# Key and value columns of two heads in one 512-column matmul

## The chip, the cores and the metric

The kernel runs on one core of a Trainium2 chip. The metric is the device time of one launch in microseconds (us), and the kernel before takes 2609.01 us, the median of three runs (2603.92 to 2610.87). TensorE (PE) multiplies; its weight loads have a row of their own in the profile (PEld). VectorE (DVE) and ScalarE (ACT) do the elementwise work, GpSimd (POOL) a little of it, and SyncE (SP) issues the transfers of the weights. PE writes its sums into eight banks of 512 fp32 columns, which DVE and ACT read.

## The reference, cut to what matters

Two layers run one after the other on 256 tokens of width 2048. The first has a modulation (adaln) of the norms, neighbourhood attention over 256 latent and 256 context tokens, an output projection and a convolutional FFN. The second has an mLSTM, a latent causal attention and gated output projections. The change is in the first attention's projections:

```python
def project(t):                                  # t: h (256 tokens), then hc (256 tokens)
    q, k, v = jnp.split(t @ w_qkv, 3, axis=-1)   # w_qkv is 2048 x 6144
    sh = (t.shape[0], t.shape[1], NA_HEADS, HEAD_DIM)          # 16 heads of 128
    return rms_norm(q.reshape(sh), q_g), rms_norm(k.reshape(sh), k_g), v.reshape(sh)
q, k, v = project(h)
qc, kc, vc = project(hc)
...
s_lat = einsum('bqhd,bkhd->bhqk', qb, kb) * scale + bias       # masked outside the window
s_ctx = einsum('bqhd,bchd->bhqc', qb, kc) * scale
p = softmax(concatenate([s_lat, s_ctx], -1))
o = einsum('bhqk,bkhd->bqhd', p[..., :nk], vb) + einsum('bhqc,bchd->bqhd', p[..., nk:], vc)
```

Everything is fp32. The kernel splits each fp32 operand into a high and a low part and sums three products (high by high, high by low, low by high).

## The kernel before, in words

**Units of weights.** Every weight matrix is laid out in blocks of 1 MB. A `Unit` (L179) is one block: SP loads it into one of three `raw` tiles, ACT copies it to a rounded tile `whi`, and DVE subtracts to get `wlo`. That is done in two halves ("subs") of 128x1024, each in one of five pairs of buffers, up to four subs ahead of PE (`AHEAD`). Between them stand "rest" units, whose weights (`w_ada`) DVE multiplies and sums into `acc` without PE.

**The projections.** `na_units` (L973) lists the units. The eight pairs of heads are eight groups. Group 0 is woven into the adaln units. For each of groups 1 to 7 there are two units for the keys (`na_k`, L762), two for the values (`na_v`, L818) and two for the queries (`na_q`, L842). Keys and values are needed for 512 tokens, four tiles of 128, and queries for two tiles. `GemmX` (L492) keeps a token tile of `hH` or `hL` as the stationary operand and streams the 256 weight columns of the two heads: `mm3` (L259) issues three matmuls of 256 columns for each of 16 depth steps and each token tile. Two token tiles share a bank. So one group has 16 x 4 x 3 = 192 matmuls for the keys, as many for the values and 96 for the queries.

**After a product.** A key tile is squared on ACT for its norm (`evac` in `na_k`). When all four are done, `chain` runs once per head: DVE and ACT compute the norm's factors (`rsqrt`), ACT copies the four scaled tiles to `kx`, PE transposes them, ACT copies the transposed tile to `k` and DVE takes its low part. The banks of the keys come free when both heads' copies to `kx` are done. A value tile goes to `v` in two pieces, one per head, by ACT and DVE. The queries take a like path (`na_qnorm`, L852), and then `na_attn` (L892) computes scores, softmax, transposes of `p`, and the product with `v`, while the projections of the next group run.

**What sets the order.** Nothing is scheduled on the chip: each engine has a fixed list of instructions. A planner writes the lists while it builds the program. It keeps a clock of its own for PE (`self.now`), ACT and DVE, with costs per instruction. The product of the unit at hand is written in pieces, and at each `yield` of its body the planner looks (`poll`, L382) whether any other piece of work is due by its clock, and writes that next. For the projections the `yield` stands after a token tile of a sub, 12 matmuls. `bank()` (L243) takes a free bank; where none is free, `need` (L230) first writes the work that will free one.

**After the projections** the first weights of the output projection (`wo_units`, L1115) follow. `o_split` (L1109) turns the heads that are done from `oF` into `o`, high and low, on ACT and DVE; PE needs them in the order of the heads.

Of the kernel before, what the change touches and what calls it, by code (L numbers as in the profile page):

```python
# [78 lines left out]
def blocks():  # L79


    t = {}

    def grid(name, K, kt, spans):
        for span in spans:
            for k0 in range(0, K, kt):
                t.setdefault(name, []).append((k0, min(kt, K - k0), span if isinstance(span[0], tuple) else (span,)))

    def wide(lo, hi, n=512):
        return [(c, min(n, hi - c)) for c in range(lo, hi, n)]  # L90
    grid("w_ada", KD, 8, wide(0, 2 * D, 256))
    grid("w_ada", KD, 4, wide(2 * D, 6 * D))
    grid("na_w_qkv", KD, 4, [(c, 256) for c in (0, D, 2 * D)])
    grid("na_w_qkv", KD, 8, [(c + 256 * g, 256) for c in (0, D, 2 * D) for g in range(1, 8)])
    for c in (0, FF):
        grid("ffn_w_up", KD, 8, wide(c, c + FF - 128, 256))
        grid("ffn_w_up", KD, 16, [(c + FF - 128, 128)])
    grid("ffn_w_down", KF, 8, wide(0, D, 256))
    grid("w_in_2", KD, 8, wide(0, 2048, 256))
    grid("w_in_2", KD, 4, wide(2048, 4096))  # L100
    grid("w_in_2", KD, 8, wide(4096, 6144, 256) + wide(6160, 9232, 256) + wide(9296, 15440, 256))
    grid("w_uq_2", 4, 4, wide(0, 3072, 384))
    grid("w_ukv_2", 4, 4, wide(0, 4096))
    grid("na_w_o", KD, 4, wide(0, D // 2))
    grid("na_w_o", KD, 8, wide(D // 2, D, 256))
    for name in ("w_a_2", "w_b_2", "w_out_2"):
        grid(name, KD, 8, wide(0, D, 256))
    return t
# [391 lines left out]
        self.k.mm3(self.out[j], xh, xl, self.wcols(hi), self.wcols(lo), b.start(), last)  # L500


def tokens(x, cg):

    return x[cg].rearrange("p (k c) -> p k c", k=4)
# [22 lines left out]
class Model(Kern):  # L528
# [152 lines left out]
    def na_setup(self):  # L681
        nc = self.nc
        p = self.L.push("h")
        self.hH = p.tile([128, KD, 512], F32R, name="hH")
        self.hL = p.tile([128, KD, 512], F32R, name="hL")
        self.h_ready = set()
        p = self.R.push("kqv")
        self.accring = Ring(self, self.p_c, "acc", [128, 512], F32, 1)
        self.qring = Ring(self, p, "q", [128, 2, 512], F32R, 1)
        self.kring = Ring(self, p, "k", [128, 2, 512], F32R, 2)  # L690
        self.ccring = Ring(self, self.p_c, "cc", [128, 32], F32, 8)
        self.vring = Ring(self, p, "v", [128, 2, 4, 128], F32R, 2)
        self.kxring = Ring(self, p, "kx", [128, 512], F32, 2)
        self.tring = self.kxring
        self.sqring = Ring(self, p, "sq", [128, 512], F32, 1)
        self.q, self.k, self.v, self.rq, self.bias = {}, {}, {}, {}, {}
        self.v_ready, self.k_ready, self.q_ready, self.o_ready = {}, set(), set(), set()
        p = self.R.push("nx")
        self.nx = p.tile([128, KD, 512], F32, name="nx")
        self.adaS = [p.tile([4, 256], F32, name=f"adaS{j}") for j in range(2)]  # L700
        self.x_done, self.x_scaled = 0, set()
        self.rawx = p.tile([128, 2048], F32, name="rawx")
# [59 lines left out]
    def na_k(self, heads):  # L762
        n = 128 * len(heads)
        per = 512 // n
        st = {"r": [], "n": 0, "e": 0}

        def done(j, out, b, last):
            if j == 0:
                st["c"] = self.ccring.get()
            if j % per == 0:  # L770
                st["r"].append(self.releaser(b, per * len(heads)))

            def evac():
                yield from self.calm()
                c = st["c"][0]
                junk, i = self.kxring.get()
                for x in range(len(heads)):
                    self.act(junk[:, col(x)], out[:, col(x)], AF.Square, accum_out=c[:, 4 * x + j:4 * x + j + 1])
                self.kxring.put(i)
                yield  # L780
                st["e"] += 1
                if st["e"] == 4:
                    for x in range(len(heads)):
                        self.spawn(chain(x), 0.2 * x)
            st[j] = out
            self.spawn(evac(), 0.2)

        def chain(x):
            c, ci = st["c"]
            cx, cxi = self.ccring.get()  # L790
            yield from self.rsqrt(cx[:, 0:4], c[:, 4 * x:4 * x + 4], HD, cx[:, 4:12])
            yield
            t, i = self.kxring.get()
            for j in range(4):
                self.act(t[:, col(j)], st[j][:, col(x)], AF.Copy, scale=cx[:, j:j + 1])
                st["r"][j // per]()
            self.ccring.put(cxi)
            st["n"] += 1
            if st["n"] == len(heads):
                self.ccring.put(ci)  # L800
            yield
            b = self.bank()
            for j in range(4):
                self.tr(b.t[:, col(j)], t[:, col(j)])
            self.kxring.put(i)
            yield 0.2
            h = heads[x]
            self.k[h] = self.kring.get()
            k = self.k[h][0]
            self.act(k[:, 0], b.t, AF.Copy, scale=self.vec("kg", 0))  # L810
            yield
            self.stt(k[:, 1], b.t, self.vec("kg", 0), k[:, 0].bitcast(F32), ALU.mult, ALU.subtract)
            b.free()
            self.k_ready.add(h)
        return GemmX(self, KD, 4, lambda k, j: (self.hH[:, k, col(j)], self.hL[:, k, col(j)]), lambda w: w, n, done,
                     need=lambda k: self.need(lambda: k in self.h_ready))

    def na_v(self, heads):  # L818
        def done(j, out, b, last):
            if j == 0:  # L820
                for h in heads:
                    self.v[h] = self.vring.get()
            if not hasattr(b, "rel") or j % 2 == 0:
                b.rel = self.releaser(b, 2)

            def evac(rel=b.rel):
                yield from self.calm()
                o = out.rearrange("p (h c) -> p h c", h=2)
                for i, h in enumerate(heads):
                    v = self.v[h][0]  # L830
                    self.A.copy(out=v[:, 0, j], in_=o[:, i])
                yield
                for i, h in enumerate(heads):
                    v = self.v[h][0]
                    self.V.tensor_sub(out=v[:, 1, j], in0=o[:, i], in1=v[:, 0, j])
                    self.v_ready[h] = self.v_ready.get(h, 0) + 1
                rel()
            self.spawn(evac(), 0.2 + 0.3 * j)
        return GemmX(self, KD, 4, lambda k, j: (self.hH[:, k, col(j)], self.hL[:, k, col(j)]), lambda w: w, 256, done,
                     need=lambda k: self.need(lambda: k in self.h_ready))  # L840

    def na_q(self, heads):  # L842
        outs = []

        def done(j, out, b, last):
            outs.append(out)
            if j:
                self.spawn(self.na_qnorm(heads, outs, b), 0.2)
        return GemmX(self, KD, 2, lambda k, j: (self.hH[:, k, col(j)], self.hL[:, k, col(j)]), lambda w: w, 256, done,
                     need=lambda k: self.need(lambda: k in self.h_ready))  # L850

    def na_qnorm(self, heads, outs, b):  # L852

# [36 lines left out]
        return hb, i  # L890

    def na_attn(self, h):  # L892
        self.need(lambda: h in self.k_ready and self.v_ready.get(h) == 4 and h in self.bias)
        hb, hi_ = self.bias.pop(h)
        x = h % 2
        q, k, r = self.q[h][0], self.k[h][0], self.rq[h][0]
# [59 lines left out]
            ss[t].free()  # L956
        yield
        b = self.bank()
        v = self.v[h][0]
        for x in range(4):  # L960
            self.mm3(b.t[:, 0:256], v[:, 0, x], v[:, 1, x], pt[:, 0, x], pt[:, 1, x], x == 0, x == 3)
        self.ptring.put(pti)
        self.vring.put(self.v.pop(h)[1])
        yield 0.2
        if self.oH is None:
            self.A.copy(out=self.oF[:, h], in_=b.t[:, 0:256])
# [6 lines left out]
    def na_units(self):  # L973
# [15 lines left out]
        rest.reverse()  # L989
        for g in range(1, 8):  # L990
            heads = [2 * g, 2 * g + 1]
            for c0, job in ((D, self.na_k(heads)), (2 * D, self.na_v(heads)), (0, self.na_q(heads))):
                for ku in range(2):
                    us.append(Unit(self.source("na_w_qkv", ku * 8, 8, c0 + g * 256, 256), 8, 256, job.body(ku * 8)))
                    for _ in range(min(len(rest), 1 + ku if c0 else 1 - ku)):
                        us.append(rest.pop())

        last = [u for u in us if u.body is not None and u.kt == 4 and u.cols == 256][-1]
        last.post = self.after_h
# [697 lines left out]
    def mla_begin(self):  # L1697
# [10 lines left out]
        self.kring = Ring(self, p, "bk", [128, 2, 512], F32R, 2)  # L1708
        self.qrring = Ring(self, p, "bqr", [128, 2, 256], F32R, 2)
        self.krring = Ring(self, p, "bkr", [128, 2, 256], F32R, 2)  # L1710
        self.vring = Ring(self, p, "bv", [128, 2, 2, 256], F32R, 2)
        self.zring = Ring(self, p, "bz", [128, 256], F32, 6)
        self.sqring = Ring(self, p, "bsq", [128, 2, 2, 192], F32, 2)
# [440 lines left out]
```

## Time and profile before

| what | value |
|---|---|
| median of three runs | 2609.01 us |
| the profiled execution | 2611.98 us |
| its span, first to last instruction | 2610.2 us |
| mean granted TensorE clock | 0.995 |
| PE busy in the span | 2550.1 us (98%) |
| DVE, ACT busy | 1844.4 us (71%), 1420.7 us (54%) |

The span is the profiled execution without 1.8 us around it. A busy time is the union of an engine's instructions; matmuls overlap in their pipeline, so a single one shows 283 ns (256 columns) while the next starts much earlier. How fast PE really goes is read from starts, not from durations. Groups 1 to 7 of the projections run from about 175 to 645 us, with the attention of the groups before written in between.

### The profile page before, as it was taken

The numbers are of one execution on the slowest core, as the hardware profiler recorded it, in microseconds if no ns is written. First come the engines' busy times: TensorE is split into PE (matmuls) and PEld (weight loads), VectorE is DVE, ScalarE is ACT, GpSimd is POOL, SyncE is SP. The second block draws the span as 40 slices with busy tenths as digits, with TensorE's granted clock in tenths as the row PEclk, the third lists the DMA queues.
The fourth block names the chain that finished last, engine by engine and source line by source line (L and its number), as shares of the span: only waits on it lengthen the run. The fifth ranks groups of instructions, "written<-read, shape, count | busy, mean of one in ns | idle before, by whom it ended". The sixth has DMA issues, their size and how long they took to land.

```text
span 2610.2 us, 40676 instructions
## 1 busy us (share of the span) xinstructions
PE 2550.1 (98%) x16038; PEld 2268.7 (87%) x16038; DVE 1844.4 (71%) x3027; ACT 1420.7 (54%) x2617; POOL 241.3 (9%) x263
## 2 busy tenths in 40 slices
PE   4999999999989999999999999999999999999999
PEld 2799999999978888888888888888888888888888
DVE  7987777677677888787555568677665576677664
ACT  5664444344555555555444456667554467775442
POOL 5421111111110000000000050000000000000000
PEclk9999999999999999999999999999999999999999
DMA  7876776676556666666566554554555553345553
GB/s 267 297 259 221 197 247 189 195 221 182 202 183 225 222 230 225 212 232 219 183 210 208 194 191 163 184 186 158 181 187 200 205 175 134 121 142 209 201 202 147
DMA packets 82543, 522.37 MB, mean 200 GB/s; under 512 B 9232, under 2 KB 15376, under 8 KB 23856
## 3 DMA queue, kind: packets, MB, share of 16 engines
q1 hardware_dynamic: 76656, 501.88, 54.1%
q0 software_dynamic: 5696, 17.90, 4.1%
q8 instruction: 126, 2.06, 0.3%
q14 instruction: 65, 0.53, 0.1%
HBM read 511.35 MB, written 8.39 MB: 199 GB/s over the span
## 4 chain that ended last, share of the span: by engine, by line
PE 94%; DVE 4%; ACT 1%; issue 1%; DMA 0%; SPq 0%; DVEq 0%; ACTq 0%
PE bank L256 91%; PE bank L265 2%; DVE wlo L151 2%; DVE hL L151 0%; ACT L149 0%; DMA nx<-in_ctxT_dram 0%; ACT whi L151 0%; SPq L707 0%; DVE hf L151 0%; DVE gb L151 0%; DVE mct L151 0%; DVE cc L151 0%; DVE adaC L151 0%; PE bank L608 0%; DVE acc L151 0%
## 5 line engine op out<-in xcount | busy, mean ns | idle before, releaser
L151 DVE TENSOR_TENSOR wlo<-raw,whi 128x1024 fp32r<-128x1024 f32 (+3 forms) x822 | 983.3, 1208 | 236.4 <-ACT whi L151 232.2
L151 ACT CAST whi<-raw 128x1024 fp32r<-128x1024 f32 (+3 forms) x822 | 830.5, 1021 | 422.4 <-PE bank L256 321.8
L256 PE MATMUL bank<-h,whi 128*128 128x512 f32 (+1 forms) x1696 | 593.9, 395 | 0.0
L256 PE MATMUL bank<-hf,whi 128*128 128x512 f32 x1376 | 485.0, 397 | 2.6 <-DVE hf L151 2.6
L256 PE MATMUL bank<-h,wlo 128*128 128x256 f32 x1680 | 470.7, 280 | 0.0
L256 PE MATMUL bank<-hf,wlo 128*128 128x256 f32 x1376 | 386.9, 281 | 0.0
L256 PEld LDWEIGHTS bank<-h,whi 128*128 128x128 f32 x1696 | 317.2, 188 | 71.9
L256 PE MATMUL bank<-whi,hH 128*128 128x256 f32 x1280 | 367.1, 287 | 0.0
L256 PE MATMUL bank<-whi,hL 128*128 128x256 f32 x1280 | 362.8, 283 | 2.2 <-DVE hL L151 2.2
L256 PE MATMUL bank<-wlo,hH 128*128 128x256 f32 x1280 | 362.8, 283 | 1.2 <-DVE wlo L151 1.2
L256 PEld LDWEIGHTS bank<-h,wlo 128*128 128x128 f32 x1680 | 317.4, 189 | 0.5 <-DVE wlo L151 0.3
L256 PEld LDWEIGHTS bank<-hf,whi 128*128 128x128 f32 x1376 | 259.0, 188 | 64.7 <-DVE hf L151 3.9
L256 PEld LDWEIGHTS bank<-hf,wlo 128*128 128x128 f32 x1376 | 261.1, 190 | 0.0
L256 PEld LDWEIGHTS bank<-whi,hL 128*128 128x128 f32 x1280 | 245.7, 192 | 2.5 <-DVE hL L151 2.4
L256 PEld LDWEIGHTS bank<-wlo,hH 128*128 128x128 f32 x1280 | 245.8, 192 | 2.3 <-DVE wlo L151 1.8
L256 PEld LDWEIGHTS bank<-whi,hH 128*128 128x128 f32 x1280 | 245.7, 192 | 1.0
L256 PE MATMUL bank<-hid,whi 128*128 128x512 f32 x688 | 243.1, 399 | 0.0
L256 PE MATMUL bank<-hid,wlo 128*128 128x256 f32 x688 | 193.2, 281 | 0.0
L151 DVE SCALAR_TENSOR_TENSOR acc<-raw,cs,acc 128x512 f32<-128x512 f32 x240 | 186.8, 778 | 6.8
L256 PEld LDWEIGHTS bank<-hid,whi 128*128 128x128 f32 x688 | 129.3, 188 | 32.2
L151 ACT COPY fold<-bank 128x256 f32<-128x256 f32 x118 | 43.6, 372 | 160.9 <-PE bank L256 158.2
L256 PEld LDWEIGHTS bank<-hid,wlo 128*128 128x128 f32 x688 | 130.0, 189 | 0.0
(334 smaller groups left out, 3695.7 us busy)
## 6 DMA issues: line engine op xcount, KB each, us to landing
raw<-in_w_in_dram SPq DMA_DIRECT2D x120, 1024.0 KB, 4.8
raw<-in_w_ada_dram SPq DMA_DIRECT2D x86, 1024.0 KB, 4.9
raw<-in_ffn_w_up_dram SPq DMA_DIRECT2D x86, 1024.0 KB, 4.9
raw<-in_na_w_qkv_dram SPq DMA_DIRECT2D x42, 1024.0 KB, 4.9
raw<-in_ffn_w_down_dram SPq DMA_DIRECT2D x40, 1024.0 KB, 4.9
raw<-in_na_w_o_dram SPq DMA_DIRECT2D x16, 1024.0 KB, 5.0
raw<-in_w_a_dram SPq DMA_DIRECT2D x16, 1024.0 KB, 5.0
raw<-in_w_b_dram SPq DMA_DIRECT2D x16, 1024.0 KB, 4.9
```

The lines of the kernel that those rows point to most:

```text
L151: r = f(*a, **kw)
L256: self.T.matmul(out, lhsT, rhs, start=start, stop=stop)
L265: self.T.transpose(out, in_, self.con("id"))
```

## The change

The weight blocks of groups 1 to 7 hold 256 key columns and 256 value columns side by side, four depth steps per block. There are four such units a group in place of two for keys and two for values. A new `GemmKV` streams all 512 columns past a stationary token tile: one triple of 512-column matmuls in place of two triples of 256. Each of the four token tiles has a bank of its own, taken when the tile is first reached, and a `yield` stands after every depth step (three matmuls). A bank comes free after three releases: the value piece, and both heads' copies of the key piece. Values of both heads lie in one tile of 256 columns, so a value tile is one ACT and one DVE instruction instead of two of each. Group 0 keeps its separate units with the new value tile. The queries' units are unchanged, and stand behind the four units of their group as before.

```diff
+    grid("na_w_qkv", KD, 8, [(256 * g, 256) for g in range(1, 8)])
+    grid("na_w_qkv", KD, 4, [((D + 256 * g, 256), (2 * D + 256 * g, 256)) for g in range(1, 8)])
...
+class GemmKV(GemmX):
+    def __init__(self, k, K, xs, done, need):
+        super().__init__(k, K, 4, xs, lambda w: w, 512, done, need)
+    def body(self, kbase):
+        def run(k0, nk, hi, lo):
+            if self.banks is None:
+                self.banks = [None] * 4
+            for j in range(4):
+                if self.banks[j] is None:
+                    self.banks[j] = self.k.bank()
+                b = self.banks[j]
+                self.out = {j: b.t}
+                for kk in range(nk):
+                    kc = kbase + k0 + kk
+                    self.nd(kc)
+                    self.step(j, kc, hi[:, kk], lo[:, kk], b, kc == self.K - 1)
+                    yield
+                if kbase + k0 + nk == self.K:
+                    self.done(j, b.t, b, True)
+                    yield
+        return run
...
-        self.vring = Ring(self, p, "v", [128, 2, 4, 128], F32R, 2)
+        self.vring = Ring(self, p, "v", [128, 2, 4, 256], F32R, 1)
...
             for j in range(4):
                 self.act(t[:, col(j)], st[j][:, col(x)], AF.Copy, scale=cx[:, j:j + 1])
-                st["r"][j // per]()
+                st["r"][j]()
...
+    def na_values(self, j, out, heads, rel):
+        g = heads[0] // 2
+        yield from self.calm()
+        if g not in self.v:
+            self.v[g] = self.vring.get()
+        v = self.v[g][0]
+        self.A.copy(out=v[:, 0, j], in_=out)
+        yield
+        self.V.tensor_sub(out=v[:, 1, j], in0=out, in1=v[:, 0, j])
+        self.v_ready[g] = self.v_ready.get(g, 0) + 1
+        rel()
...
+    def na_kv(self, heads):
+        evac = self.na_keys(heads)
+        def done(j, out, b, last):
+            rel = self.releaser(b, 3)
+            self.spawn(self.na_values(j, out[:, 256:512], heads, rel), 0.2)
+            self.spawn(evac(j, out[:, 0:256], rel), 0.3)
+        return GemmKV(self, KD, self.hx, done, self.hneed)
...
-            for c0, job in ((D, self.na_k(heads)), (2 * D, self.na_v(heads)), (0, self.na_q(heads))):
-                for ku in range(2):
-                    us.append(Unit(self.source("na_w_qkv", ku * 8, 8, c0 + g * 256, 256), 8, 256, job.body(ku * 8)))
-                    for _ in range(min(len(rest), 1 + ku if c0 else 1 - ku)):
-                        us.append(rest.pop())
+            job = self.na_kv(heads)
+            for ku in range(4):
+                us.append(Unit(self.source("na_w_qkv", ku * 4, 4, D + g * 256, 512), 4, 512, job.body(ku * 4)))
+                for _ in range(min(len(rest), 1 + ku % 2)):
+                    us.append(rest.pop())
+            job = self.na_q(heads)
+            for ku in range(2):
+                us.append(Unit(self.source("na_w_qkv", ku * 8, 8, g * 256, 256), 8, 256, job.body(ku * 8)))
+                for _ in range(min(len(rest), 1 - ku)):
+                    us.append(rest.pop())
```

**PE, the keys of group 3 (heads 6 and 7).** `kx1` and `kx0` are the scaled keys of the two heads, `cons` the identity for a transpose; the banks carry the planner's numbers. Before, the transposes stand in the middle of the value product:

```order
L256 MATMUL bank0_3795<-whi_3779,hL_107 128x256
L265 MATMUL bank5_4037<-cons_76,kx1_126 128x128 x4
L256 MATMUL bank0_3795<-whi_3779,hH_106 128x256
L256 MATMUL bank0_3795<-wlo_3780,hH_106 128x256
...
L265 MATMUL bank3_4055<-cons_76,kx0_125 128x128 x4
L256 MATMUL bank1_3794<-whi_3808,hH_106 128x256
```

After, they stand behind the queries' product (`bank4_3489`) and inside the first sub of the next group's keys and values:

```order
L257 MATMUL bank4_3489<-whi_3502,hL_107 128x256
L266 MATMUL bank7_3629<-cons_76,kx1_125 128x128 x4
L257 MATMUL bank3_3634<-whi_3536,hH_106 128x512
L257 MATMUL bank3_3634<-wlo_3537,hH_106 128x512
...
L257 MATMUL bank1_3649<-whi_3536,hH_106 128x512
...
L257 MATMUL bank7_3662<-whi_3536,hH_106 128x512
...
L257 MATMUL bank6_3673<-whi_3536,hL_107 128x512
L266 MATMUL bank5_3677<-cons_76,kx0_124 128x128 x4
L257 MATMUL bank6_3673<-whi_3536,hH_106 128x512
```

So the transposes moved from the second half of the values to the boundary between two groups, and the third bank of the new group (`bank7_3662`) is the one that `kx1`'s transposes used 12 matmuls earlier (`bank7_3629`).

**ACT, from the last squares of group 3's keys to its copies into `kx`.** Before (`pt` and `oF` belong to the attention of the group before, `cc` are the norm's factors):

```order
L151 ACTIVATE kx0_125,cc1_116<-bank4_3481 128x128 x2
L151 CAST pt1_1894<-bank5_3862 128x4x128
L151 CAST pt1_1894<-bank3_3867 128x4x128
L151 ACTIVATE cc4_119<-cc4_119 128x4 x2
L151 COPY oF_1892<-bank7_3894 128x256
L151 ACTIVATE cc6_121<-cc6_121 128x4 x2
L151 CAST whi_3974<-raw_3844 128x1024
L151 CAST whi_3990<-raw_3844 128x1024
L151 ACTIVATE kx1_126<-bank2_3480,cc4_119 128x128 x2
```

The same stretch after the change (`sq0` are the queries, squared and copied):

```order
L152 CAST v0_123<-bank2_3097 128x256
L152 ACTIVATE kx0_124,cc3_118<-bank2_3097 128x128 x2
L152 CAST whi_3536<-raw_3420 128x1024
L152 ACTIVATE cc5_120<-cc5_120 128x4 x2
L152 CAST whi_3569<-raw_3420 128x1024
L152 ACTIVATE cc6_121<-cc6_121 128x4 x2
L152 ACTIVATE kx1_125<-bank6_3058,cc5_120 128x128
...
L152 CAST whi_3638<-raw_3522 128x1024
L152 ACTIVATE k0_113<-bank7_3629,vecs_75 128x512
L152 ACTIVATE sq0_126,cc0_115<-bank4_3489 128x128 x4
L152 ACTIVATE kx0_124<-bank6_3058,cc6_121 128x128
```

The attention's instructions are gone from this stretch; the second head's copies now stand behind the queries' four squares.

**ACT, the first subs of the output projection.** Before, the weights of its fifth sub (`whi_7448`) stand behind nine of the copies to `o`:

```order
L151 CAST o_7352<-oF_1892 128x256 x2
L151 ACTIVATE sq0_127,cc7_122<-bank7_7221 128x128 x4
L151 CAST o_7352<-oF_1892 128x256 x4
L151 COPY sq0_127<-bank7_7221 128x512
L151 CAST o_7352<-oF_1892 128x256 x3
L151 CAST whi_7448<-raw_7241 128x1024
```

After, it is already the fourth sub (`whi_6019`) whose weights stand behind nine copies to `o`, and behind the two keys of the last group as well:

```order
L152 CAST o_5931<-oF_1887 128x256
L152 ACTIVATE k0_113<-bank2_5917,vecs_75 128x512
L152 CAST o_5931<-oF_1887 128x256 x2
L152 ACTIVATE sq0_126,cc7_122<-bank1_5784 128x128 x4
L152 CAST o_5931<-oF_1887 128x256
L152 ACTIVATE k1_114<-bank0_5965,vecs_75 128x512
L152 CAST o_5931<-oF_1887 128x256 x3
L152 COPY sq0_126<-bank1_5784 128x512
L152 CAST o_5931<-oF_1887 128x256 x2
L152 CAST whi_6019<-raw_5717 128x1024
```

The last group's key copies came into the start of the output projection. From the FFN on, the lists of all engines are the same but for the numbers of banks, and SP's and POOL's lists are the same throughout.

## Rows read from the trace of the kernel before

**Rows 1.** The page: busy time by engine, and chain of waits by engine.

```profile
PE 2550.1 (98%) x16038; PEld 2268.7 (87%) x16038; DVE 1844.4 (71%) x3027; ACT 1420.7 (54%) x2617; POOL 241.3 (9%) x263
...
PE 94%; DVE 4%; ACT 1%; issue 1%; DMA 0%; SPq 0%; DVEq 0%; ACTq 0%
```

**Rows 2.** Windows: us, PE PEld DVE ACT POOL, granted clock, DMA, GB/s.

```profile
195.00:645.00 450.00, 449.98 (x3698) 446.05 (x3696) 328.12 (x572) 193.28 (x519) 73.70 (x78) 1.00 0.68 208
740.00:760.00 20.00, 12.44 (x54) 9.66 (x53) 13.78 (x25) 8.46 (x17) 6.94 (x8) 0.74 0.41 152
1532.00:1545.00 13.00, 13.00 (x59) 10.78 (x58) 6.34 (x7) 5.80 (x7) 8.41 (x14) 1.00 0.64 237
```

**Rows 3.** Waits, 160 to 700 us: total us, times, longest.

```profile
ACT whi L151 <- PE bank L256: 37.3, 23, 4.6
ACT whi L151 <- DMA raw<-in_na_w_qkv_dram: 32.4, 16, 5.4
PE bank L256 <- ACT o L151: 0.4, 1, 0.4
```

**Rows 4.** Groups of instructions (part 5 of the page): PE in the projections.

```profile
L256 PE MATMUL bank<-whi,hH 128*128 128x256 f32 x1280 | 367.1, 287 | 0.0
```

**Rows 5.** Timeline, PE, keys and values: start, duration, instruction, count.

```profile
362.03 0.28 PE L256 MATMUL bank<-whi,hH 128*128 128x256 f32 x1
...
376.91 0.28 PE L256 MATMUL bank<-wlo,hH 128*128 128x256 f32 x1
```

**Rows 6.** Timeline, PE, the mLSTM values, 512 columns.

```profile
1531.95 0.39 PE L256 MATMUL bank<-wlo,h 128*128 128x512 f32 x1
...
1544.87 0.39 PE L256 MATMUL bank<-wlo,h 128*128 128x512 f32 x1
```

**Rows 7.** Timeline, ACT, norms of keys: group 0, then group 3.

```profile
166.66 0.30 ACT L151 ACTIVATE kx<-bank 128x128 f32<-128x128 f32 x1
...
172.82 2.18 ACT L151 ACTIVATE kx<-bank,cc 128x128 f32<-128x128 f32 x8
...
340.20 0.30 ACT L151 ACTIVATE kx<-bank 128x128 f32<-128x128 f32 x1
...
349.88 2.17 ACT L151 ACTIVATE kx<-bank,cc 128x128 f32<-128x128 f32 x8 [0.36 <-DVE cc L151]
```

**Rows 8.** Groups of instructions by form, 195 to 645 us: ACT, then DVE.

```profile
L151 ACT CAST v<-bank 128x128 fp32r<-128x128 f32 x56 | 10.8, 281 | 23.0 <-PE bank L256 23.0
L151 ACT ACTIVATE k<-bank,vecs 128x512 fp32r<-128x512 f32 x14 | 9.5, 687 | 15.4 <-PE bank L265 15.1
...
L151 ACT COPY oF<-bank 128x256 f32<-128x256 f32 x14 | 5.2, 373 | 24.2 <-PE bank L256 24.1
...
L151 DVE SCALAR_TENSOR_TENSOR acc<-raw,cs,acc 128x512 f32<-128x512 f32 x168 | 132.1, 786 | 4.8
...
L151 DVE SCALAR_TENSOR_TENSOR k<-bank,vecs,k 128x512 fp32r<-128x512 f32 x14 | 10.4, 748 | 5.0 <-ACT k L151 5.0
```

**Rows 9.** Timeline: PE at scores and transposes of keys, DVE ahead of scores.

```profile
323.50 0.86 PE L256 MATMUL bank<-k,q 128*128 128x512 f32 x3
...
357.22 0.60 PE L265 MATMUL bank<-cons,kx 128*128 128x128 f32 x4
...
323.01 0.74 DVE L151 SCALAR_TENSOR_TENSOR q<-bank,qgs,q 128x512 fp32r<-128x512 f32 x1
```

**Rows 10.** Timeline, start of the output projection: ACT, DVE, PE.

```profile
644.90 0.71 ACT L151 CAST o<-oF 128x256 fp32r<-128x256 f32 x2 [1.71 <-PE bank L256]
...
649.59 1.05 ACT L151 CAST whi<-raw 128x1024 fp32r<-128x1024 f32 x1
...
652.27 1.22 DVE L151 TENSOR_TENSOR wlo<-raw,whi 128x1024 fp32r<-128x1024 f32 x1
...
655.40 0.28 PE L256 MATMUL bank<-o,wlo 128*128 128x256 f32 x1
...
658.28 0.28 PE L256 MATMUL bank<-o,wlo 128*128 128x256 f32 x1
```

More of the change, by code (lines that the diff above doesn't have):

```diff
@@ L93, in blocks @@
     grid("na_w_qkv", KD, 4, [(c, 256) for c in (0, D, 2 * D)])
-    grid("na_w_qkv", KD, 8, [(c + 256 * g, 256) for c in (0, D, 2 * D) for g in range(1, 8)])
+    grid("na_w_qkv", KD, 8, [(256 * g, 256) for g in range(1, 8)])
+    grid("na_w_qkv", KD, 4, [((D + 256 * g, 256), (2 * D + 256 * g, 256)) for g in range(1, 8)])
     for c in (0, FF):
@@ L764, in na_k, with hx, hneed, na_keys @@
         per = 512 // n
-        st = {"r": [], "n": 0, "e": 0}
+        evac = self.na_keys(heads)
         def done(j, out, b, last):
-            if j == 0:
-                st["c"] = self.ccring.get()
[L770 to L776, printed above, removed]
-                for x in range(len(heads)):
[L778 to L786, printed above, removed]
+            if j % per == 0:
+                b.rel = self.releaser(b, per * len(heads))
+            self.spawn(evac(j, out, b.rel), 0.2)
+        return GemmX(self, KD, 4, self.hx, lambda w: w, n, done, need=self.hneed)
+    def hx(self, k, j):
+        return self.hH[:, k, col(j)], self.hL[:, k, col(j)]
+    def hneed(self, k):
+        self.need(lambda: k in self.h_ready)
+    def na_keys(self, heads):
+        st = {"r": [None] * 4, "n": 0, "e": 0}
+        def evac(j, out, rel):
+            if "c" not in st:
+                st["c"] = self.ccring.get()
+            st["r"][j], st[j] = rel, out
+            yield from self.calm()
+            c = st["c"][0]
+            junk, i = self.kxring.get()
+            for x in range(len(heads)):
+                self.act(junk[:, col(x)], out[:, col(x)], AF.Square, accum_out=c[:, 4 * x + j:4 * x + j + 1])
+            self.kxring.put(i)
+            yield
+            st["e"] += 1
+            if st["e"] == 4:
+                for x in range(len(heads)):
+                    self.spawn(chain(x), 0.2 * x)
         def chain(x):
@@ L814, in chain @@
             self.k_ready.add(h)
-        return GemmX(self, KD, 4, lambda k, j: (self.hH[:, k, col(j)], self.hL[:, k, col(j)]), lambda w: w, n, done,
-                     need=lambda k: self.need(lambda: k in self.h_ready))
+        return evac
+    def na_values(self, j, out, heads, rel):
+        g = heads[0] // 2
+        yield from self.calm()
+        if g not in self.v:
+            self.v[g] = self.vring.get()
+        v = self.v[g][0]
+        self.A.copy(out=v[:, 0, j], in_=out)
+        yield
+        self.V.tensor_sub(out=v[:, 1, j], in0=out, in1=v[:, 0, j])
+        self.v_ready[g] = self.v_ready.get(g, 0) + 1
+        rel()
     def na_v(self, heads):
         def done(j, out, b, last):
[L820 to L823, printed above, removed]
+            if j % 2 == 0:
                 b.rel = self.releaser(b, 2)
[L826 to L840, printed above, removed]
+            self.spawn(self.na_values(j, out, heads, b.rel), 0.2 + 0.3 * j)
+        return GemmX(self, KD, 4, self.hx, lambda w: w, 256, done, need=self.hneed)
+    def na_kv(self, heads):
+        evac = self.na_keys(heads)
+        def done(j, out, b, last):
[3 more added lines that the diff above has]
+        return GemmKV(self, KD, self.hx, done, self.hneed)
     def na_q(self, heads):
@@ L848, in done @@
                 self.spawn(self.na_qnorm(heads, outs, b), 0.2)
-        return GemmX(self, KD, 2, lambda k, j: (self.hH[:, k, col(j)], self.hL[:, k, col(j)]), lambda w: w, 256, done,
-                     need=lambda k: self.need(lambda: k in self.h_ready))
+        return GemmX(self, KD, 2, self.hx, lambda w: w, 256, done, need=self.hneed)
     def na_qnorm(self, heads, outs, b):
@@ L892, in na_attn @@
     def na_attn(self, h):
-        self.need(lambda: h in self.k_ready and self.v_ready.get(h) == 4 and h in self.bias)
+        self.need(lambda: h in self.k_ready and self.v_ready.get(h // 2) == 4 and h in self.bias)
         hb, hi_ = self.bias.pop(h)
@@ L958, in na_attn @@
         b = self.bank()
-        v = self.v[h][0]
+        v, c = self.v[h // 2][0], col(h % 2)
         for x in range(4):
-            self.mm3(b.t[:, 0:256], v[:, 0, x], v[:, 1, x], pt[:, 0, x], pt[:, 1, x], x == 0, x == 3)
+            self.mm3(b.t[:, 0:256], v[:, 0, x, c], v[:, 1, x, c], pt[:, 0, x], pt[:, 1, x], x == 0, x == 3)
         self.ptring.put(pti)
-        self.vring.put(self.v.pop(h)[1])
+        self.v_left[h // 2] = self.v_left.get(h // 2, 2) - 1
+        if not self.v_left[h // 2]:
+            self.vring.put(self.v.pop(h // 2)[1])
         yield 0.2
@@ L1710, in mla_begin @@
         self.krring = Ring(self, p, "bkr", [128, 2, 256], F32R, 2)
+        self.v_left = {}
         self.vring = Ring(self, p, "bv", [128, 2, 2, 256], F32R, 2)
```

## The prediction

> **What bounds the kernel now.** I read the busy times of the page first, then its chain of waits. PE is busy for 98% of the span, and 94% of the chain that ended last is PE; DVE has 4% of the chain and ACT 1% [rows 1]. That is an average over stages, so the next view was the table by windows. In the stretch of the changed projections, 195 to 645 us, PE is busy for 449.98 of 450 us at a granted clock of 1.00, while DVE has 328 us, ACT 193 us, and the DMA engines 0.68 of their time [rows 2]. The third view was the list of waits: between 160 and 700 us PE waited once, for 0.4 us. ACT waited often, among others 16 times and 32.4 us in all for weights of this matrix, 5.4 us at the longest [rows 3]. PE never felt it, since the weights are made up to four subs ahead. So this stage lasts as long as PE's list of instructions lasts, and a change there is worth what it takes off that list, less any wait that it brings to PE.
>
> **The change: the pace of PE.** A triple of the projections has three kinds of matmuls; the first kind stands 1280 times [rows 4], which is 8 groups of heads times 160 triples. Of the 160 triples of a group, 64 are keys and 64 are values, so groups 1 to 7 have 7 x 128 = 896 such triples, 2688 matmuls of 256 columns. After, they are 1344 matmuls of 512. The duration in a row (287 ns) is no pace, since matmuls overlap; I take starts. From 362.03 to 376.91 us PE issued 124 matmuls of 256 columns with nothing between: 14.88 / 124 = 0.1200 us each [rows 5]. The trace has 512-column matmuls in the same pattern of three, with a loaded tile of 128 columns, in the mLSTM's values: from 1531.95 to 1544.87 us there are 19 triples, 57 matmuls, 12.92 / 57 = 0.2267 us each [rows 6]. So twice the columns cost 0.1067 us more, and 0.0133 us of each matmul doesn't depend on the columns. A pair of 256 becomes one of 512: 2 x 0.1200 - 0.2267 = 0.0133 us, times 1344 = 17.9 us, or 2.56 us a group. Bounds for this term: nothing speaks for more than the 17.9 us, and at the least it is 0, if the new matmuls take 0.2400. I take the whole, since rows 6 are the same pattern at the same clock.
>
> The Trainium skill ("TensorE: Matmul & The Clock Gate", section "Wait — 56ns, not 53.3ns?") gives a fixed cost of only 2.5 ns a matmul at the full clock. By it the saving would be an estimated 1344 x 2.5 ns = 3.4 us. The trace disagrees by its 13.3 ns, and I go by the trace. The same page's section "A second HAM failure mode: psum-queue depth-cycling" speaks against the change: a kernel with 512-column matmuls that cycled through its banks idled often enough for the clock to swing. Here the stretch 1532 to 1545 us, which has 512 columns and changes banks, shows PE busy for 13.00 of 13.00 us at a granted clock of 1.00; the clock falls (0.74) where PE is busy for 12.44 of 20 us [rows 2]. So I put no term for it.
>
> **ACT and DVE.** Value tiles: per group eight ACT copies of 0.281 us become four, by the nearest row of 256 columns 0.373 us each [rows 8]: 2.25 to 1.49 us. DVE's subtractions halve in number alike. Neither is on the path. PE's list gets some 4% shorter in the stage, so DVE's share goes from 73% to 76% and DMA's 0.68 to about 0.71. The number of weight casts and transfers is the same, SP's and POOL's order is the same, so the lead of the weights should last; I cost this at 0.
>
> **What is late next: the boundaries.** Keys and values now end together, and the queries are the only cover for the norm of the keys. Let T0 be the end of the last key and value matmul. The queries take 96 x 0.120 = 11.5 us, then PE comes to the transposes of `kx1`. Before, the chain from the first of the last tile's squares to the last copy to `kx` took 166.66 to 175.00 = 8.3 us in group 0, without attention between, and 340.20 to 349.88 + 2.17 = 352.05, 11.9 us, in group 3, with attention's work between [rows 7]. After, attention's work is gone from that stretch of ACT's list, so it is the 8.3 us that apply, for both heads even, and 3.2 us are left: no wait.
>
> Then the tight places. (a) The third bank of the next group's keys and values is the one that `kx1`'s transposes used. They take 0.60 us [rows 9], `k` takes 0.687 us on ACT and 0.748 on DVE [rows 8], together 2.04 us. PE gets to that bank after the transposes and 12 matmuls of 0.2267: 0.60 + 2.72 = 3.32 us. So 1.3 us are left. One `acc` instruction of 0.786 us [rows 8] ahead of the `k` subtraction on DVE still fits; a block of four, 3.1 us, comes 1.9 us late. (b) `kx0`'s transposes come after 21 matmuls: 0.60 + 4.76 = 5.4 us behind the queries. On ACT stand `k0`, four squares of the queries and four copies of `kx0` (2.18 / 8 = 0.27 us each) between: 0.60 + 0.69 + 4 x 0.30 + 1.09 = 3.6 us, or 4.6 with a cast `whi` of 1.05 us [rows 7, 8, 10]. About 1 us is left. (c) The scores need `q`, which DVE finished at 323.75, while PE came to the scores at 323.50 [rows 9]; that place was tight before, and an `acc` block can make it late again. So a boundary costs between 0 and about 1.9 us, seven of them 0 to 13 us. I take 0.2 us each, 1.4 us, as the slack of rows covers all but a block that falls badly.
>
> (d) Output projection. Before, the fifth sub's low part was done at 652.27 + 1.22 = 653.5, and PE used it at 658.28 us: 4.8 us ahead; the copies to `o` before its cast began at 644.90, the cast at 649.59 [rows 10]. After, the fourth sub stands there, used at 655.40, and the two keys add 1.37 us on ACT and 1.50 on DVE: it is ready at 654.9 to 656.4. The transposes of these keys stand ahead of its use, 2 x 0.60 us, so it is wanted at 656.6. The margin is 0.2 to 1.7 us; a block of 3.1 us on DVE would turn it into a wait of up to 3 us. Bounds 0 to 3 us, I take 0.6.
>
> **Sum.** -17.9 + 1.4 + 0.6 = -15.9 us against the profiled execution of 2611.98 us: 2596.1 us. The median of the runs is 2.97 us below the profiled one: 2609.01 - 15.9 = 2593 us. With no wait at all it is 2591.1; the runs of before lie up to 5 us below their median, so this case's own range is 2587 to 2599.
>
> **Rivals.** A: the boundaries eat much of the gain. DVE's `acc` blocks or attention's work fall between `k` and its bank in most groups, 1 to 2 us each; at 1.5, 7 x 1.5 = 10.5 us, and the time is 2609.0 - 17.9 + 10.5 = 2601.6 us. For it: slacks of about 1 us where before there were several. Against: PE waited for none of its producers here, though (c) is as tight already.
>
> B: slower. ACT's list is in order, and a `whi` cast that waits for its transfer now stands ahead of `k0` and of `kx0`'s copies. Before, such a wait was hidden by the lead of weights; after, it holds back the third bank, and PE with it. Of the longest wait, 5.4 us [rows 3], 1.3 us fit in the slack: 4.1 x 7 = 28.7 us, time 2609.0 - 17.9 + 28.7 = 2619.8 us. It decides from 17.9 / 7 = 2.6 us a boundary. For it: 16 such waits before, two a group. Against: their mean is 2.0 us, most would have to fall just there, and a PE that waits lets the transfers catch up.
>
> C: the change doesn't do what it says, since 512 columns in this stage don't go at the pace of rows 6: with stationary tiles that change for every token tile the pair saves a fifth, 0.0027 us, and the gain is 1344 x 0.0027 = 3.6 us: 2605.4 us. The Trainium skill's 2.5 ns, named above, would come to nearly the same. Against: rows 6 are the same instructions on the same engine, and there the loaded tile changes as often.
>
> **How the numbers follow.** Forecast 0.68, A 0.20, B 0.09, C 0.03. The forecast is 2593 us. The range 2587 to 2606 takes in the forecast's own range, A and C, and leaves out B and a little beside it. About 0.3%, 7.8 us, is what a measurement of this kernel can tell from no change: faster is below 2601.2 us, slower above 2616.8. Faster: 0.66 of the forecast and 0.09 of A, 0.75. Same: the rest of these two and C, 0.16. Slower: B, 0.09.
>
> **What would show it.** PE has 16038 - 1344 = 14694 matmuls, a triple of keys and values starts every 0.68 us, and the output projection starts some 16 us sooner. Waits of PE at the boundaries for DVE's `k` or for ACT's `kx` of over 1 us each show A; the same waits behind an ACT that waits for `raw` show B. A pace of 0.235 us or more shows C. A granted clock below 1.00 between 195 and 630 us would show that I was wrong to leave the clock out; a wait of PE for weights there, that their lead doesn't last.

## The result, and the profile after

The changed kernel takes 2592.4 us (median of seven runs), the kernel before 2609.01 us beside it (seven runs too): a ratio of 0.994, with an interval of 0.9927 to 0.9954. A second series gave 2595.85 against 2607.86 us, 0.9962 (0.9949 to 0.9974). The two intervals meet at 0.995, some 13 us. The forecast was 2593 us.

The page of the changed kernel, its row of busy times and its chain by engine, against [rows 1]:

```profile
PE 2530.4 (98%) x14694; PEld 2198.0 (85%) x14694; DVE 1842.5 (71%) x2995; ACT 1418.7 (55%) x2585; POOL 241.4 (9%) x263
...
PE 92%; DVE 4%; ACT 2%; DMA 1%; issue 1%; SPq 0%; DVEq 0%; ACTq 0%
```

The matmuls are 16038 - 1344 = 14694, as worked out. PE still has nearly the whole chain. The window of the changed stage (columns as in [rows 2]):

```profile
195.00:630.00 435.00, 433.80 (x2422) 376.64 (x2420) 327.60 (x545) 189.15 (x488) 73.89 (x82) 1.00 0.71 215
```

PE is busy for 433.80 of 435 us at a granted clock of 1.00, and DMA has the 0.71 that the prediction named. The wait of ACT for weights, 160 to 700 us, against [rows 3] (total us, times, longest):

```profile
ACT whi L152 <- DMA raw<-in_na_w_qkv_dram: 63.8, 26, 8.1
```

Those of PE alone in the same stretch:

```profile
PE bank L266 <- ACT p L152: 0.9, 1, 0.9
PE bank L257 <- DVE wlo L152: 0.7, 1, 0.7
PE bank L257 <- DVE q L152: 0.3, 2, 0.2
PE bank L257 <- ACT o L152: 0.2, 1, 0.2
```

PE waits 2.1 us in all, where it waited 0.4; the prediction had put 2.0 for new waits. ACT's waits for weights doubled (32.4 to 63.8 us) and PE felt almost none of it.

What the stage lost is read between two places that both kernels have: the first product with `hH` and the first with `hf`, the start of the FFN. One row of each kernel for either place, first `hH`, then `hf` (a group of matmuls: least, middle and greatest duration in ns, first and last start):

```profile
L256 PE MATMUL bank<-whi,hH x33: 281/283/582, 66.3 to 94.7; 128*128 128x256 f32 x33
...
L256 PE MATMUL bank<-hf,whi x207: 391/398/794, 753.8 to 830.0; 128*128 128x512 f32 x104
```

```profile
L257 PE MATMUL bank<-whi,hH x35: 278/283/416, 65.6 to 94.8; 128*128 128x256 f32 x35
...
L257 PE MATMUL bank<-hf,whi x249: 391/391/796, 740.3 to 829.7; 128*128 128x512 f32 x125
```

The first product with `hH` starts at 66.3 us before and 65.6 after. So the way to the FFN took 753.8 - 66.3 = 687.5 us before and 740.3 - 65.6 = 674.7 after: 12.8 us less. The second profile of the changed kernel gives 742.4 - 67.0 = 675.4, 12.1 us less. (Counted from the first matmul of group 1, at 175.0 us before and at 174.4 and 177.1 after, the two are 12.9 and 13.5 us less.) That agrees with the middle of the two intervals. The span of the first pair of profiles fell by 22.1 us (2610.2 to 2588.1). Of the other 9 us, 4.6 came in the FFN's down product and 3.4 behind it, where the instructions are the same in both kernels; the last section shows the 4.6.

### The profile page after: what moved, and what is told of

It is laid out like the page before. It is cut to its first block, busy times and chain, and to the rows that moved or that the text cites. A ratio compares the mean times of both kernels' runs of the same rounds, so it can differ in the third digit from the quotient of the medians.

```text
span 2588.1 us, 37928 instructions
## 1 busy us (share of the span) xinstructions
PE 2530.4 (98%) x14694; PEld 2198.0 (85%) x14694; DVE 1842.5 (71%) x2995; ACT 1418.7 (55%) x2585; POOL 241.4 (9%) x263
## 4 chain that ended last, share of the span: by engine, by line
PE 92%; DVE 4%; ACT 2%; DMA 1%; issue 1%; SPq 0%; DVEq 0%; ACTq 0%
PE bank L257 90%; PE bank L266 2%; DVE wlo L152 2%; DVE acc L152 1%; ACT whi L152 0%; DMA raw<-in_na_w_qkv_dram 0%; ACT L150 0%; DVE hL L152 0%; DMA nx<-in_ctxT_dram 0%; DMA raw<-in_w_ada_dram 0%; SPq L734 0%; DVE gb L152 0%; DVE mct L152 0%; ACT o L152 0%; ACT kx L152 0%
## 5 line engine op out<-in xcount | busy, mean ns | idle before, releaser
L257 PE MATMUL bank<-whi,hH 128*128 128x512 f32 (+1 forms) x832 | 287.8, 346 | 0.0
L257 PE MATMUL bank<-whi,hL 128*128 128x512 f32 (+1 forms) x832 | 284.3, 342 | 2.2 <-DVE hL L152 2.2
L257 PE MATMUL bank<-wlo,hH 128*128 128x512 f32 (+1 forms) x832 | 284.2, 342 | 1.2 <-DVE wlo L152 1.2
L257 PEld LDWEIGHTS bank<-whi,hL 128*128 128x128 f32 x832 | 158.1, 190 | 20.5 <-DVE hL L152 2.4
L257 PEld LDWEIGHTS bank<-wlo,hH 128*128 128x128 f32 x832 | 158.3, 190 | 18.0 <-DVE wlo L152 1.8
L257 PEld LDWEIGHTS bank<-whi,hH 128*128 128x128 f32 x832 | 158.2, 190 | 16.6
```

The lines of the kernel that those rows point to most:

```text
L257: self.T.matmul(out, lhsT, rhs, start=start, stop=stop)
```

## The experiments

My theory: the gain is PE's pace, 0.0133 us per pair of matmuls, less some 2 us of new waits at the places that the prediction named. The rival: it comes from the new order and the fewer value pieces.

**The pair undone, the order kept.** `GemmKV` issues each product as two of 256 columns; the lists of ACT and DVE are the same, and PE's but for the doubled matmuls.

```diff
+    def step(self, j, kc, hi, lo, b, last):
+        xh, xl = self.xs(kc, j)
+        o, s = self.out[j], b.start()
+        self.k.mm3(o[:, 0:256], xh, xl, hi[:, 0:256], lo[:, 0:256], s, False)
+        self.k.mm3(o[:, 256:512], xh, xl, hi[:, 256:512], lo[:, 256:512], False, last)
```

> The order of every engine as in the changed kernel, but each 512-column matmul of keys and values is issued as two of 256 columns into the two halves of the same bank (2688 in place of 1344). Theory (the gain is the pace of PE, 0.0133 us saved per pair): the stage gets 17.9 us longer again, 2592 + 18 = 2610 us, ratio to the kernel before 0.998 to 1.003. Rival (the gain comes from the new order, with fewer value pieces on ACT and DVE and the attention's work out of the keys' chain): the time stays near 2592, ratio 0.994.

Measured: 2611.19 us against 2607.49 before, ratio 1.0012 (1.0001 to 1.0023). The whole gain is gone, so the rival falls. The stage shows it too (the start of the FFN, with `hH` first at 66.5 us):

```profile
L257 PE MATMUL bank<-hf,whi x197: 387/398/794, 757.1 to 829.7; 128*128 128x512 f32 x197
```

757.1 - 66.5 = 690.6 us. By these single profiles the order alone costs 3.1 us against the kernel before (687.5); the pairing alone gives 15.9 us against the changed kernel (674.7), 0.0118 us a pair where I had 0.0133. Of the 3.1 us, 1.9 are waits of PE that the profile shows: 2.3 us between 160 and 700 us here (1.0 for `q`, 0.7 for `wlo`, 0.4 for `pt`, 0.2 for `o`), 0.4 before. The rest isn't traced.

**The interleaving made coarser.** One yield per token tile of a sub, after its first triple, in place of one after each triple.

```diff
-                    yield
+                    if kk == 0:
+                        yield
```

> The changed kernel with a yield after every second depth step's place (once per token tile of a sub, after its first triple) in place of after each triple, so other work is put between the products at half as many places. Theory (interleaving finely is no part of the gain): 2590 to 2596 us, ratio 0.993 to 0.996, PE's waits between 195 and 630 us still under 3 us. Rival (the fine yields keep PE's insertions and the releases of banks in time): PE's waits grow by 5 us or more, 2597 us or above, ratio 0.996 or more.

Measured: 2596.44 us, ratio 0.9952 (0.9937 to 0.9967), which holds the changed kernel's values. The waits of PE between 195 and 630 us:

```profile
PE bank L257 <- ACT kx L152: 2.7, 4, 0.7
PE bank L266 <- ACT p L152: 0.7, 1, 0.7
```

They sum to 3.4 us, a little over the 3 that were expected: PE now waits at four boundaries for a bank that the second head's copies to `kx` set free. From `hH` (65.7) to the FFN (742.9) it took 677.2 us, some 2 us more than in the two profiles of the changed kernel. By these single profiles the fine yields are worth some 2 us, which the total doesn't resolve.

**Cut at 384 and 128 columns.** The same edit as the first, with cuts at 384. The planner put the other work at other places here than in the first experiment, so the order isn't quite kept; PE's waits between 160 and 700 us came to 4.0 us.

> As the split into two halves, but cut at 384 and 128 columns. It tells what the 0.0133 us are. Theory (a cost per matmul that doesn't depend on its width): 384 take 0.160 + 0.013, 128 take 0.053 + 0.013, together 0.240 as two of 256, so 2610 us like the split into halves. Rival (a matmul is never shorter than some 0.11 us, as the transposes of 128 columns that start every 0.11 us in the trace): 0.173 + 0.11 = 0.283 us a pair, 1344 x 0.043 = 58 us more than the halves, 2668 us.

Measured: 2679.69 us, ratio 1.0276 (1.0259 to 1.0294). The rival holds in the main, though the time is 12 us above its 2668. Two triples in the timeline of PE (start, duration, instruction, count):

```profile
300.91 0.40 PE L257 MATMUL bank<-whi,hH 128*128 128x384 f32 x1
301.14 0.34 PE L257 MATMUL bank<-wlo,hH 128*128 128x384 f32 x1
301.32 0.34 PE L257 MATMUL bank<-whi,hL 128*128 128x384 f32 x1
301.49 0.22 PE L257 MATMUL bank<-whi,hH 128*128 128x128 f32 x1
301.55 0.27 PE L257 MATMUL bank<-wlo,hH 128*128 128x128 f32 x1
301.66 0.28 PE L257 MATMUL bank<-whi,hL 128*128 128x128 f32 x1
301.77 0.39 PE L257 MATMUL bank<-whi,hH 128*128 128x384 f32 x1
```

The 384 columns start 0.17 to 0.18 us apart: 0.160 for the columns (0.1067 per 256) and 0.015. The 128 columns would take 0.067 each by a cost per matmul. The first of the three takes 0.06, the others 0.11, and the first wide one after them 0.23 in place of 0.17, so that the three cost 0.34 together, 0.11 each. Six matmuls take 301.77 - 300.91 = 0.86 us, where two triples of 256 take 0.72. So 13 to 15 ns a matmul hold for 256, 384 and 512 columns, but three narrow matmuls in a row, each with a weight load of its own, cost no less than some 0.11 us each in this stream. The Trainium skill ("TensorE: Matmul & The Clock Gate", section "LDWEIGHTS (loading the stationary operand)") gives the time of a weight load in ns as its columns / 1.2, so for 128 columns an estimated 106.7 ns. The trace's 0.11 us agrees with that. That the load is the cause isn't shown, since no run had fewer loads; nor is it shown whether the 13 ns belong to a matmul or to its load, as the change halves both.

**More time before the bank is free.** One copy more of each transposed key to `k`, then six more, given to ACT without telling the planner's clock. The order is the same but for the added rows.

```diff
+            for _ in range(1):        # 6 in the second kernel
+                self.A.e.activation(out=k[:, 0], in_=b.t, func=AF.Copy, scale=self.vec("kg", 0))
             self.act(k[:, 0], b.t, AF.Copy, scale=self.vec("kg", 0))
```

> The changed kernel with one more copy of each transposed key tile to k on ACT (0.689 us, twice a group), the order of all else unchanged. In the trace of the changed kernel the bank of kx1 is free 2.11 us after its transposes began, and PE wants it some 3.3 us after: 1.2 us of slack. Theory (that slack, and kx0's lead of 1.2 to 1.4 us): 2.80 us, still no wait of PE for k at the six boundaries between groups; only the output projection, which had no slack left, waits 2 x 0.69 = 1.4 us longer than its 0.65. Some 2594 us. Rival (the slack is nominal, the bank is wanted sooner or other work falls between): waits of 0.3 us or more at each boundary.

Measured with one more: 2597.32 us, one run, so no verdict on the total. The waits of PE between 195 and 630 us:

```profile
PE bank L257 <- DVE q L152: 2.0, 4, 0.5
PE bank L266 <- ACT p L152: 1.1, 1, 1.1
```

No wait for `k`: the slack of over 0.69 us is there. The scores wait more often for `q`, which the expectation had not named. The output projection waited 1.4 us for `wlo` and 0.9 for `o`, where the changed kernel waited 0.7 and 0.2: 1.4 us longer, as expected.

> The same with six more copies: 4.13 us more before the bank of kx1 is free, so 6.24 us after its transposes, wanted at 3.3. Theory: PE waits some 2.9 us for DVE's k at each of six boundaries, 17.6 us, kx0's copies have 4.13 - 2.9 us to make up from their 1.3 and wait little, and the output projection waits 8.3 us more: 2592 + 26 = 2618 us, the whole gain gone, and the lead of weights hides the rest. Rival (the bank's late release hides behind other banks or the weights' queue): under 10 us more, below 2602 us.

Measured with six more: 2657.19 us, ratio 1.0192 (1.0179 to 1.0205). The waits in the same stretch:

```profile
PE bank L257 <- DVE k L152: 18.8, 6, 3.2
PE bank L257 <- DVE q L152: 9.0, 3, 3.9
PE bank L266 <- ACT p L152: 0.5, 1, 0.5
```

Six waits for `k` of 18.8 us in all, against six of 17.6 expected. So the place and the slack are right. The total was 39 us above my 2618. PE's waits ahead of this stretch (160 to 195 us) and behind it (683 to 760 us):

```profile
PE bank L266 <- ACT sq L152: 5.8, 1, 5.8
...
PE bank L257 <- ACT o L152: 5.8, 2, 4.5
PE bank L257 <- DVE wlo L152: 2.6, 1, 2.6
```

The output projection's 8.4 us, 7.5 more than in the changed kernel, are about the 8.3 that I had put for it. What I had not counted are the 9.0 us for `q`, the 5.8 for the queries' squares `sq`, and the clock, which fell after some of the stalls. The whole stretch, windows around its first stall, and one behind its third (the granted clock is the third number from the end):

```profile
195.00:683.00 488.00, 458.34 (x2457) 392.96 (x2456) 334.30 (x555) 239.60 (x563) 77.62 (x84) 0.97 0.64 198
...
250.00:254.00 4.00, 1.00 (x5) 0.49 (x3) 0.69 (x1) 3.80 (x10) 0.00 (x0) 1.00 0.00 0
254.00:258.00 4.00, 3.88 (x15) 3.20 (x15) 1.37 (x4) 3.17 (x10) 0.00 (x0) 0.57 0.00 0
258.00:262.00 4.00, 4.00 (x22) 3.30 (x21) 0.76 (x2) 3.61 (x6) 0.00 (x0) 1.00 0.60 190
...
331.00:335.00 4.00, 4.00 (x20) 3.26 (x21) 1.47 (x2) 3.94 (x12) 0.00 (x0) 1.00 0.00 0
```

PE stood for 3.12 us before 254.12. The granted clock was 0.57 for the next 4 us, most of them at the level of 1.2 GHz (matmuls of 512 columns started at 254.71 and 255.14, 0.43 us apart), and then 1.00 again. After a stall of the same 3.12 us that ended at 330.91 it stayed at 1.00. A wait of 3 us thus costs 3 us, and at some places more. From the granted 0.97, against 1.00 in the changed kernel, I estimate 0.03 x 488 = 15 us for the clock. That leaves some 9 of the 39 us unexplained.

**Group 0 paired too.** The first pair of heads, whose products stand between the adaln units, gets the same units of 512 columns.

```diff
...
-    FIRST = (2, 5, 8)
+    FIRST = (3, 8)            # (2, 5) in the second kernel
...
-        g0 = [(D, self.na_k([0, 1])), (2 * D, self.na_v([0, 1])), (0, self.na_q([0, 1]))]
+        g0 = [(D, 512, self.na_kv([0, 1])), (0, 256, self.na_q([0, 1]))]
```

> The changed kernel with the first pair of heads (group 0, woven into the adaln units) paired in the same way: 192 matmuls of 512 columns there in place of 384 of 256. Theory (PE's list sets the time wherever PE is busy): 192 x 0.0133 = 2.6 us less, 2590 us. Rival (up to 175 us PE waits for the hidden tiles and for weights, so a shorter list gains nothing, and units of 1 MB come later than two of half a MB): 2592 to 2600 us, with longer PE waits before 175 us.

Measured: 2618.85 us, ratio 1.0042 (1.0026 to 1.0058), some 25 us worse than the changed kernel. The rival holds, and by more than I gave it. PE's waits between 40 and 200 us (in the changed kernel 8.3 us in ten waits for `wlo`, and 2.2 for `hL`):

```profile
PE bank L257 <- DVE wlo L152: 25.7, 17, 5.4
PE bank L257 <- ACT sq L152: 2.3, 1, 2.3
```

The clock fell as well: the granted clock was 0.94 from 76 to 205 us, where the changed kernel had 0.99. By these two numbers that is an estimated 0.05 x 129 = 6 us.

> Group 0 paired too, but with its units put two adaln units after the first and five after (keys and values, queries), so that the hidden tiles' products start behind as many adaln products as in the changed kernel (160, not 176). Theory 1 (what the first try lost is the place of its units): 2588 to 2594 us. Theory 2 (1 MB units and their 512-column products between the adaln units delay the adaln products, on which the next hidden tiles wait, wherever they are put): 2600 us or more.

Measured: 2593.87 us, ratio 0.9958 (0.9944 to 0.9973). The place of the units was most of the loss, as theory 1 has it. But nothing is gained either:

```profile
PE bank L257 <- DVE wlo L152: 16.3, 24, 3.3
PE bank L266 <- ACT kx L152: 1.3, 1, 1.3
PE bank L257 <- ACT sq L152: 0.3, 1, 0.3
```

PE waits 24 times for weights. The profile of the changed kernel has 8.3 us of such waits in this stretch, its second profile 11.8. From the first product with `hH` to the FFN it took 746.3 - 66.0 = 680.3 us, 5 us more than in the changed kernel, with 192 matmuls less. Where PE waits for others, a shorter list was worth nothing here. No version here beats the changed kernel.

## Why the prediction was right, point by point

**The bound.** PE's list set the time of the stage: with the pair undone in the same order, the gain went. That step is shown.

**The pace.** I put 0.0133 us a pair, 17.9 us; the experiment gives 15.9. This is the term that was sized too large, by 2 us. Where the product runs undisturbed, the pace is that of [rows 6]; behind an insertion it isn't. Two stretches of the changed kernel's timeline, the first behind the transposes of `kx1`:

```profile
305.06 0.48 PE L257 MATMUL bank<-whi,hH 128*128 128x512 f32 x1
305.38 0.40 PE L257 MATMUL bank<-wlo,hH 128*128 128x512 f32 x1
...
307.69 0.39 PE L257 MATMUL bank<-whi,hL 128*128 128x512 f32 x1
307.92 0.39 PE L257 MATMUL bank<-whi,hH 128*128 128x512 f32 x1
```

```profile
280.96 0.39 PE L257 MATMUL bank<-whi,hH 128*128 128x512 f32 x1
...
283.22 0.39 PE L257 MATMUL bank<-wlo,hH 128*128 128x512 f32 x1
```

The ten matmuls from 280.96 take 0.226 us each. Behind the transposes the first takes 0.32 and the ten after it (305.38 to 307.69) 0.231 each. In the kernel with the pair undone, the 256 columns went back to 0.120 within two matmuls of an insertion (310.25, 310.37, 310.49). I had taken the pace from two stretches without insertions. Summed over the 66 insertions from group 1 on, the first matmuls cost 3.8 us more than at 0.2267 in the changed kernel, against 3.3 more than at 0.1200 with the pair undone; the second to tenth cost 1.4 more, against 0.4 less. That makes 2.3 us, about the 2 that are missing. I can't say why the wider matmuls take longer to settle.

**The boundaries.** At the tight places the hand walk held to some 0.4 us. The timeline of ACT and DVE at the same boundary:

```profile
297.56 1.13 ACT L152 ACTIVATE kx<-bank,cc 128x128 f32<-128x128 f32 x4
...
305.35 0.69 ACT L152 ACTIVATE k<-bank,vecs 128x512 fp32r<-128x512 f32 x1 [3.93 <-PE bank L266]
...
307.39 1.14 ACT L152 ACTIVATE kx<-bank,cc 128x128 f32<-128x128 f32 x4
```

```profile
306.07 0.75 DVE L152 SCALAR_TENSOR_TENSOR k<-bank,vecs,k 128x512 fp32r<-128x512 f32 x1 [2.85 <-ACT k L152]
```

`kx1` was ready at 298.69, 6.0 us before its transposes at 304.71. I had worked out 3.2, with a chain of 8.3 us that counts the copies of both heads; here those of `kx0` came only behind the queries' squares. Its bank was free at 306.82, 2.11 us after (2.04 worked out), and PE came to it at 307.92, 3.2 us after (3.32 worked out): 1.1 us of slack. `kx0` was ready at 308.53, 1.4 us ahead of its use at 309.96 (1 worked out). The six added copies show that the slack is real and ends where it should. So rival A did not come, and rival B neither: ACT waited twice as long for `raw`, yet PE never waited for `k` or `kx` at a boundary. The Trainium skill (page "TensorE: Matmul & The Clock Gate", section "A second HAM failure mode: psum-queue depth-cycling") tells of a kernel with 512 columns that cycled through its banks, idled between groups of matmuls and had its clock swing. That didn't come true here: with 512 columns and four banks in turn PE was busy for 433.80 of 435 us, and the granted clock was 1.00.

**The waits that came.** I put 1.4 us for the boundaries and 0.6 for the output projection. The latter waited 0.65 us for `wlo`:

```profile
640.62 0.48 PE L257 MATMUL bank<-o,whi 128*128 128x256 f32 x2
641.76 0.38 PE L257 MATMUL bank<-o,wlo 128*128 128x256 f32 x1 [0.65 <-DVE wlo L152]
```

At the scores `q` was late twice, 0.3 us, as place (c) said. The third wait, 0.9 us for `p` at 200.68, is one I had not named: a transpose of `acc` took a bank that ACT was to read for the softmax, and that softmax stood on DVE behind sums into `acc` that had waited for a transfer of 7.6 us (186.81 to 194.42 in the chain). In the second profile that wait was 0.3. The order alone cost 3.1 us in the experiment, against the 2.0 that I put.

**The sum.** -15.9 (pairing) + 3.1 (order) = -12.8 us for the stage, against -17.9 + 2.0 = -15.9 predicted. The median hit the forecast more closely than the stage did; that the first series lies at -16.6 and the second at -12.0 us is the spread of runs, not a merit of the sum. So the hit to 1 us is luck: the pairing was sized 2 us too large and the order 1.1 us too small. Rival C is ruled out: of the 17.9 us, 15.9 are there, and the 1344 new matmuls of the stage took 0.231 us each from a start to the next, under the 0.235 that would have shown C.

## What to carry to other kernels

Where PE is busy without a gap, count matmuls: here two of 256 columns cost some 12 ns more than one of 512, and a narrow one of 128 cost as much as one of some 230 would (0.11 us, at 0.0133 and 0.1067 per 256). Where PE waits for weights or for its operands, the same pairing gained nothing, and where its coarser units of weights stood decided 25 us (2618.85 against 2593.87). Before widening an output over more banks, walk the boundary: what frees the bank that PE wants next, and by how much it is early, could be read here from the trace before to some tenths of a us.

## What the runs showed that I had not expected

**One program, two paces.** The FFN's down product has the same instructions in both kernels. The profile before and the one after, near 1300 us:

```profile
1299.88 0.40 PE L256 MATMUL bank<-hid,whi 128*128 128x512 f32 x1
1300.12 0.28 PE L256 MATMUL bank<-hid,wlo 128*128 128x256 f32 x1
...
1302.35 0.40 PE L256 MATMUL bank<-hid,whi 128*128 128x512 f32 x1
```

```profile
1299.91 0.39 PE L257 MATMUL bank<-hid,whi 128*128 128x512 f32 x1
1300.14 0.28 PE L257 MATMUL bank<-hid,wlo 128*128 128x256 f32 x1
...
1302.33 0.39 PE L257 MATMUL bank<-hid,whi 128*128 128x512 f32 x1
```

Seven pairs take 2.47 us before and 2.42 after. Over the stage (1240.9 to 1484.0, and 1226.8 to 1465.3) that makes 243.1 against 238.5 us, and the other profiles show one or the other: 243.1 in the changed kernel's second profile, with the pair undone, with the coarser yields, with one and with six copies more, and in the second kernel with group 0 paired; 238.5 in the first kernel with group 0 paired and with the cuts at 384. The granted clock is 1.00 in both. So this stage can be 1.9% longer in one execution than in the next, at the full clock and without a wait, and the spans of one profile against another don't give the size of a change of half a per cent; the changed stretch itself, in several profiles, does. What sets the pace stays open.
